# Ten of the twenty later modulation blocks summed on TensorE instead of VectorE, in a two-layer hybrid decoder on one Trainium2 core

## The chip, the cores and the metric

The kernel runs on one core of a Trainium2 chip. A core has five engines that run their own instruction streams: TensorE (PE in the profile, with PEld for the loading of its stationary operand), VectorE (DVE), ScalarE (ACT), GpSimd (POOL) and SyncE (SP), which here only issues DMA transfers. The metric is the device time of one execution in microseconds, as the median of several runs. The profile is of one execution, and its times are from the start of that execution's span.

## The reference, cut to what matters

The sequence has 256 tokens of 2048 channels. Each of two layers has a token-mixing part (one input projection, four groups of heads, one output projection) and a gated feed-forward part; both stand between normalisations that are modulated by vectors computed from one conditioning vector `c`:

```
cond = jax.nn.silu(c)
for l in range(DEPTH):
    mods = cond @ w_ada[l] + b_ada[l]
    sh1, sc1, g1, sh2, sc2, g2 = [m[:, None, :] for m in jnp.split(mods, 6, axis=-1)]
    h = rms_norm(x, norm_pre_mix[l]) * (1.0 + sc1) + sh1
    y = token_mixing(h, positions, w_in[l], w_out[l], ...)
    x = x + g1 * rms_norm(y, norm_post_mix[l])
    h = rms_norm(x, norm_pre_ffn[l]) * (1.0 + sc2) + sh2
    y = conv_ffn(h, ffn_w_in[l], ffn_conv_w[l], ffn_w_out[l])
    x = x + g2 * rms_norm(y, norm_post_ffn[l])
```

All is f32. `cond @ w_ada[l]` is a vector of 2048 times a matrix of 2048 x 12288, 100 MB a layer.

## The kernel before

**Weights and products.** A weight tile of 128 x 1024 f32 (512 KB) comes by DMA into the pool `raw` (4 buffers, line 406, on SP's queue). ScalarE rounds it into `wh` (line 423), VectorE takes the difference `wl` (line 424), and TensorE makes three products in its rounded f32 form for each one of the reference: activations high by weights high, high by low, low by high (`mm3`, line 228 is the matmul itself). Results gather in PSUM banks: four of the pool `mm`, and two each of two pools `mx`.

**The modulation blocks.** `mods` of a layer is cut into 12 blocks of 1024 columns, blocks 0 to 3 for the first normalisation, 4 and 5 for the first gate, 6 to 9 for shift and scale of the second normalisation, 10 and 11 for the second gate. Blocks 0 to 3 of layer 0 are computed at the start on TensorE, by `ada_quarter`. The other 20 blocks are background work, made by `ada`: 16 weight tiles of 128 x 1024, one after the other, come into the pool `rawa` (2 buffers, line 475), and VectorE multiplies each by its 128 values of `cond` and adds it to an accumulator (line 462; line 460 for the first). At the end a transpose (481), a reduction (483) and eight small matmuls sum over the 128 partitions.

**Order.** `wload` and `attn_probs` call `tick`, which at set rates starts the next background tile. With `paced` (in the feed-forward parts) the tile is held behind the last weight load; without it (mixers and output projection) the scheduler that orders each engine's stream at build time is free to place it. `drain` finishes what is left of a stage's blocks before the next stage. Ten blocks are unpaced: 4, 5, 8, 6, 9, 7 of layer 0 and 8, 6, 9, 7 of layer 1; ten are paced. In the output projection (`project_out`) all four `mm` banks are held by partial sums, twice, for one half of the columns each. After it `residual` (lines 683 to 701) computes the new x and its scale on VectorE, `pre_norm` brings h into `ht` by matmuls with `diag`, and the feed-forward matmuls begin; the second half of h needs blocks 7 and 9.

Each engine takes its instructions in the order in which they were placed.

Of the kernel before, what the change touches and what calls it, by code (L numbers as in the profile page):

```python
# [12 lines left out]
F32 = mybir.dt.float32  # L13
# [4 lines left out]
ALU = mybir.AluOpType  # L18
# [3 lines left out]
P = 128  # L22
D = 2048
S = 256
KT = D // P
# [167 lines left out]
class Ker:  # L193
# [273 lines left out]
    def ada(self, l, b):  # L467
# [19 lines left out]
                self.mm(cols[32 * q:32 * q + 32, :8], self.ident2[:, 32 * i:32 * i + 32], pv[:, :, q], i == 0, i == 1)  # L487
        self.ada_out(l, b, cols[:, :8])

    def ada_quarter(self, q):  # L490

        nc = self.nc
        bank = self.mx()
        pools = ((self.rawa, "rawa"), (self.rawm, "rawm"), (self.accp, "acc"))
        free = [A_OT + 1024] + (AT[7:9] if q else []) + (AT[:4] if q < 3 else [])
        for kc in range(KT):
            n = kc % (len(free) + 6)
            if n < len(free):  # L500
                w = self.reg(free[n], 1024)(1024)
            else:
                pool, nm = pools[(n - len(free)) % 3]
                w = pool.tile([P, 1024], F32, name=nm, tag=nm)
            nc.sync.dma_start(w, self.blk("w_ada", 0, kc, 1, (q * 512, 512), (D + q * 512, 512)))
            for i in range(2):
                o = 64 * (kc % 2) + 32 * i
                self.mm(bank[o:o + 32], self.condz[:, kc], w[:, i * 512:(i + 1) * 512], kc < 2, kc >= KT - 2)
            if kc % 2 and kc < KT - 1:
                yield  # L510
        with self.first():
            r = self.small.tile([P, 512], F32, name="hf", tag="hf")
            nc.scalar.copy(r, bank)
            cols = self.mx(8)
            for c in range(4):
                self.mm(cols[:, 2 * c:2 * c + 2], r[:, c * P:(c + 1) * P], self.ident2[:, 0:64:32], True, True)
            cols = cols.rearrange("p (c i) -> p i c", i=2)
            for i in range(2):
                self.ada_out(0, 2 * i + q // 2, cols[:, i], 4 * (q % 2))

    def ada_out(self, l, b, cols, j=0):

        nc = self.nc
        n = cols.shape[-1]
        out = self.mod[:, l, b, j:j + n]
        nc.vector.tensor_tensor(out, cols, self.vs(l, "b_ada")[:, b * 8 + j:b * 8 + j + n], op=ALU.add)
        which, part, half = b // 6, b % 6 // 2, b % 2
        g = 16 * which + 8 * half + j
        if part == 1:
            nc.vector.scalar_tensor_tensor(out, out, 1.0, self.vs(l, "pre")[:, g:g + n], op0=ALU.add, op1=ALU.mult)  # L530
        elif part == 2:
            nc.vector.tensor_tensor(out, out, self.vs(l, "post")[:, g:g + n], op=ALU.mult)

    def ada_blocks(self, l, blocks):
        for b in blocks:
            yield from self.ada(l, b)
            if b % 6 == 5:
                self.gate_out(l, b // 6)
            yield
# [1247 lines left out]
```

## Time and profile before

| | |
|---|---|
| median of 3 runs (lowest, highest) | 2699.17 us (2696.71, 2700.51) |
| the profiled execution | 2692.16 us, of it span 2690.0 us |
| mean granted TensorE clock | 0.978 |
| TensorE, VectorE, ScalarE busy | 96%, 71%, 47% of the span |
| mixers and output projection, layer 0 | about 150 to 630 us |
| feed-forward, layer 0 | about 630 to 1405 us |
| mixers and output projection, layer 1 | about 1405 to 1905 us |
| feed-forward, layer 1 | about 1905 to 2690 us |

The span is from the first to the last instruction. Times inside the program are read from a profile's own clock; a matmul's end is modelled, so that the start of one matmul to the start of the next says more of the pace than its length. An f32 matmul (not rounded) stands in the trace as two records. The granted clock is a share of TensorE's full speed: 1.00 is 2.4 GHz, 0.50 is 1.2 GHz, and values between are means over a stretch with both.

### The profile page before, as it was taken

The page shows a single profiled execution, that of the slowest core. Times are in us where ns is not written, and L with a number is a line of the kernel's source. Part 1 is how long each engine was busy: PE and PEld are TensorE (multiplying, and loading weights), DVE is VectorE, ACT ScalarE, POOL GpSimd, SP SyncE. Part 2 cuts the span into 40 slices and gives each one's busy share as a digit, 9 for nine tenths or more (in the row PEclk, how much of TensorE's full clock was granted, in tenths as well). Part 3 has the DMA queues.
Part 4 walks back from the last instruction along what each step waited for, and adds up shares of the span by engine and source line. Part 5 has one row for each costly group of instructions (what it writes and reads, how often), then busy time and mean ns, then how long its engine had stood idle before and what let it go on. Part 6 is the DMA issues. An engine that isn't in the chain of part 4 may idle for free. (4 is left out here: it accounts for less than half of the span.)

```text
span 2690.0 us, 44478 instructions
## 1 busy us (share of the span) xinstructions
PE 2571.7 (96%) x17604; PEld 2285.0 (85%) x17604; DVE 1910.7 (71%) x3014; ACT 1259.9 (47%) x2002; POOL 10.1 (0%) x22
## 2 busy tenths in 40 slices
PE   7979998888999999999998999999899999999998
PEld 4568786767999999988887879888899999998886
DVE  5568867878787778776877888865776655555555
ACT  3344454555445444454545445465544444444443
POOL 0000000000000000000000000000000000000000
PEclk9989998889999999999998999999999999999999
DMA  8765756676888888876676567735587655555554
GB/s 343 313 212 198 256 197 210 220 266 216 291 297 277 289 289 298 291 242 234 229 269 216 176 218 248 254 114 180 186 283 270 209 185 183 182 184 186 185 189 147
DMA packets 171264, 620.89 MB, mean 231 GB/s; under 512 B 19440, under 2 KB 20272, under 8 KB 169520
## 3 DMA queue, kind: packets, MB, share of 16 engines
q1 hardware_dynamic: 170048, 617.00, 67.1%
q8 instruction: 138, 2.26, 0.3%
q10 hardware_dynamic: 1008, 1.06, 0.1%
q14 instruction: 70, 0.57, 0.1%
HBM read 613.75 MB, written 4.23 MB: 230 GB/s over the span
## 5 line engine op out<-in xcount | busy, mean ns | idle before, releaser
L228 PE MATMUL mm<-ht,wh 128*128 128x256 f32 x7168 | 1314.9, 284 | 6.7 <-ACT ht L423 5.8
L423 ACT CAST wh<-raw 128x1024 fp32r<-128x1024 f32 (+1 forms) x740 | 771.5, 1043 | 960.9 <-PE mm L228 785.0
L424 DVE TENSOR_TENSOR wl<-raw,wh 128x1024 fp32r<-128x1024 f32 (+1 forms) x740 | 896.6, 1214 | 404.5 <-ACT wh L423 401.0
L228 PEld LDWEIGHTS mm<-ht,wh 128*128 128x128 f32 x7168 | 1112.3, 189 | 22.8 <-issue 7.6
L228 PE MATMUL mm<-ht,wl 128*128 128x256 f32 x3584 | 1018.1, 284 | 2.4 <-DVE wl L424 2.4
L228 PEld LDWEIGHTS mm<-ht,wl 128*128 128x128 f32 x3584 | 675.3, 188 | 10.5 <-DVE wl L424 6.2
L228 PE MATMUL mm<-wh,ht 128*128 128x512 f32 (+1 forms) x1600 | 508.0, 396 | 8.0 <-ACT ht L423 4.2
L462 DVE SCALAR_TENSOR_TENSOR acc<-rawa,condc,acc 128x1024 f32<-128x1024 f32 x300 | 384.6, 1282 | 138.2 <-DMA rawa<-in_w_ada_dram 136.8
L228 PEld LDWEIGHTS mm<-wh,ht 128*128 128x128 f32 x1600 | 303.1, 191 | 72.3 <-ACT ht L423 4.5
L228 PE MATMUL mm<-wl,ht 128*128 128x512 f32 (+1 forms) x800 | 316.2, 395 | 0.0
L228 PE MATMUL mx<-arena 128*128 128x128 f32 (+9 forms) x1576 | 235.1, 320 | 18.9 <-DVE arena L373 10.0
L228 PEld LDWEIGHTS mx<-arena 128*128 128x128 f32 (+5 forms) x1576 | 164.8, 169 | 72.5 <-issue 20.4
L228 PE MATMUL mx<-wh,ht 128*128 128x512 f32 x704 | 222.3, 396 | 0.0
L228 PEld LDWEIGHTS mm<-wl,ht 128*128 128x128 f32 x800 | 152.6, 191 | 31.5 <-issue 0.2
L228 PEld LDWEIGHTS mx<-wh,ht 128*128 128x128 f32 x704 | 132.6, 188 | 32.3
L228 PE MATMUL mx<-wl,ht 128*128 128x512 f32 x352 | 139.5, 396 | 0.0
L424 DVE TENSOR_TENSOR ht<-arena,ht 128x1024 fp32r<-128x1024 f32 x52 | 63.6, 1223 | 40.4 <-ACT ht L423 40.1
L1615 DVE SCALAR_TENSOR_TENSOR arena<-mm,vec,arena 128x255 f32<-128x255 f32 (+1 forms) x176 | 78.5, 478 | 6.2 <-ACT arena L1613 5.3
L423 ACT CAST ht<-arena 128x1024 fp32r<-128x1024 f32 x52 | 54.2, 1049 | 56.1 <-PE mm L228 30.5
L228 PEld LDWEIGHTS mx<-wl,ht 128*128 128x128 f32 x352 | 66.3, 188 | 16.2
L232 PE MATMUL mx<-ident,arena 128*128 128x128 f32 (+1 forms) x328 | 59.4, 287 | 13.4 <-ACT arena L815 5.5
L232 PEld LDWEIGHTS mx<-ident,arena 128*128 128x128 f32 (+1 forms) x328 | 38.4, 144 | 29.9 <-ACT arena L815 9.8
(314 smaller groups left out, 1516.4 us busy)
## 6 DMA issues: line engine op xcount, KB each, us to landing
raw<-in_ffn_w_in_dram SPq DMA_DIRECT2D x352, 512.0 KB, 4.2
rawa<-in_w_ada_dram SPq DMA_DIRECT2D x330, 512.0 KB, 5.0
raw<-in_ffn_w_out_dram SPq DMA_DIRECT2D x176, 512.0 KB, 4.3
raw<-in_w_in_dram SPq DMA_DIRECT2D x116, 512.0 KB, 4.3
raw<-in_w_out_dram SPq DMA_DIRECT2D x64, 512.0 KB, 4.1
arena<-in_w_ada_dram SPq DMA_DIRECT2D x36, 512.0 KB, 7.8
raw<-in_w_in_dram SPq DMA_DIRECT2D x32, 426.0 KB, 3.9
rawm<-in_w_ada_dram SPq DMA_DIRECT2D x9, 512.0 KB, 9.3
```

Source lines behind the costliest of these rows:

```text
L228: self.nc.tensor.matmul(out, lhsT=lhsT, rhs=rhs, start=start, stop=stop)
L232: self.nc.tensor.transpose(out, in_, self.ident[:k, :k])
L423: self.nc.scalar.copy(hi.bitcast(F32R), src)
L424: self.last_lo = self.nc.vector.tensor_sub(lo.bitcast(F32R), src, hi)
L462: self.nc.vector.scalar_tensor_tensor(acc, w, self.condc[:, kc:kc + 1], acc, op0=ALU.mult, op1=ALU.add)
L1615: nc.vector.scalar_tensor_tensor(c[:, s:], ps[m][:, :256 - s], self.fconv(l, 2 - s, f), c[:, s:], op0=ALU.mult, op1=ALU.add)
```

## The change

Unpaced blocks are computed by a new function, `ada_te`, the paced ones as before. A tile is now the moving operand of two f32 matmuls of 128 rows by 512 columns, whose stationary operand is one column of `cond` repeated 32 times: each writes 32 equal rows of a PSUM bank. Two tiles make a pair, whose four matmuls write the four groups of 32 partitions of one `mm` bank. ScalarE copies the first pair's bank into an accumulator of 128 x 512, VectorE adds the other seven. At the end of a block four matmuls with two columns of `ident2` add the two tiles' rows and turn them into columns. Tiles rotate over three buffers, two of `rawa` and one of `acc`.

```diff
+    def ada_te(self, l, b):
+        nc = self.nc
+        acc = self.acct()[:, 0:512]
+        tiles = []
+        for kc in range(KT + 1):
+            if kc and kc % 2 == 0:
+                bank = self.mmt()
+                for n, w in enumerate(tiles):
+                    for i in range(2):
+                        o = 64 * n + 32 * i
+                        k = kc - 2 + n
+                        self.mm(bank[o:o + 32], self.condc[:, k:k + 1].to_broadcast([P, 32]), w[:, i * 512:(i + 1) * 512],
+                                True, True)
+                if kc == 2:
+                    nc.scalar.copy(acc, bank)
+                else:
+                    nc.vector.tensor_tensor(acc, acc, bank, op=ALU.add)
+                tiles = []
+            if kc < KT:
+                pool, nm = ((self.rawa, "rawa"), (self.rawa, "rawa"), (self.accp, "acc"))[kc % 3]
+                tiles.append(pool.tile([P, 1024], F32, name=nm, tag=nm))
+                nc.sync.dma_start(tiles[-1], self.blk("w_ada", l, kc, 1, (b * 1024, 1024)))
+                yield
+        cols = self.mx(8)
+        for c in range(4):
+            self.mm(cols[:, 2 * c:2 * c + 2], acc[:, c * P:(c + 1) * P], self.ident2[:, 0:64:32], True, True)
+        self.ada_out(l, b, cols, order="c i")
...
     def ada_blocks(self, l, blocks):
         for b in blocks:
-            yield from self.ada(l, b)
+            yield from (self.ada if self.paced else self.ada_te)(l, b)
```

`ada_out` takes the other order of columns by a rearranged view. Lines behind the new function stand 30 to 33 lower: `residual` is at 716 to 734, the add of a pair at 508, a tile's load at 513.

**Where it moves instructions.** TensorE, layer 0, from the last product of the output projection (`mm<-wh,ht`) to the first of the feed-forward part (`mm<-ht,wh`); rows with `diag` are `pre_norm`'s. Before:

```order
L228 MATMUL mm<-wh,ht 128x512
L228 MATMUL mx_5511<-acc,ident_126 32x8 x8
L228 MATMUL mx_5524<-diag,arena 128x128
L228 MATMUL mx_5540<-diag,arena 128x128
L228 MATMUL mx_5524<-diag,arena 128x128 x3
L228 MATMUL mx_5540<-diag,arena 128x128 x3
L228 MATMUL mx_5550<-diag,arena 128x128 x4
L228 MATMUL mx_5560<-diag,arena 128x128 x4
L228 MATMUL mm<-ht,wh 128x256 x2
L228 MATMUL mm<-ht,wl 128x256
```

In the change, the end of the same stretch; `condc` marks the matmuls of pairs, whose tiles are in `rawa` or `acc`:

```order
L228 MATMUL mm<-acc,condc 32x512 x2
L228 MATMUL mm<-rawa,condc 32x512 x4
L228 MATMUL mm<-acc,condc 32x512 x2
L228 MATMUL mm<-rawa,condc 32x512 x4
L228 MATMUL mm<-acc,condc 32x512 x2
L228 MATMUL mm<-rawa,condc 32x512 x4
L228 MATMUL mm<-acc,condc 32x512 x2
L228 MATMUL mm<-rawa,condc 32x512 x4
L228 MATMUL mm<-acc,condc 32x512 x2
L228 MATMUL mm<-ht,wh 128x256 x2
L228 MATMUL mm<-ht,wl 128x256
L228 MATMUL mm<-ht,wh 128x256 x2
```

Thirty-eight matmuls of pairs (nine pairs and half of a tenth) now stand between the output projection's last product and the feed-forward part's first, the last 26 of them (rows 1 to 9) with nothing else between.

VectorE at the same place, where `residual` computes the scale that `diag` needs. Before:

```order
L272 SCALAR_TENSOR_TENSOR cy<-ca,cy 128x1 x2
L270 SCALAR_TENSOR_TENSOR ca<-cy,cv 128x1 x2
L272 SCALAR_TENSOR_TENSOR cy<-ca,cy 128x1 x2
L270 SCALAR_TENSOR_TENSOR ca<-cy,cv 128x1 x2
L272 SCALAR_TENSOR_TENSOR cy<-ca,cy 128x1 x2
L573 TENSOR_SCALAR diag<-ident,cy 128x128 x2
L701 SCALAR_TENSOR_TENSOR arena<-arena,cy 128x512 x4
```

In the change (508 is the add of a pair, 559 the end of block 9):

```order
L272 SCALAR_TENSOR_TENSOR cy<-ca,cy 128x1 x2
L270 SCALAR_TENSOR_TENSOR ca<-cy,cv 128x1 x2
L272 SCALAR_TENSOR_TENSOR cy<-ca,cy 128x1
L508 TENSOR_TENSOR acc<-acc,mm 128x512
L272 SCALAR_TENSOR_TENSOR cy<-ca,cy 128x1
L270 SCALAR_TENSOR_TENSOR ca<-cy,cv 128x1 x2
L272 SCALAR_TENSOR_TENSOR cy<-ca,cy 128x1
L559 TENSOR_TENSOR mod<-mx_5431,vec 128x8
L272 SCALAR_TENSOR_TENSOR cy<-ca,cy 128x1
L606 TENSOR_SCALAR diag<-ident,cy 128x128 x2
L734 SCALAR_TENSOR_TENSOR arena<-arena,cy 128x512 x4
```

An add that needs a pair's matmuls now stands in the middle of the scale's chain; there is another one earlier in it.

TensorE inside the mixers of layer 1, where a projection of 426 columns runs. Before:

```order
L228 MATMUL mm<-wl,ht 128x426
L228 MATMUL mm<-wh,ht 128x426 x2
L228 MATMUL mm<-wl,ht 128x426
L228 MATMUL mm<-wh,ht 128x426 x2
L228 MATMUL mm<-wl,ht 128x426
L228 MATMUL mm<-wh,ht 128x426 x2
L228 MATMUL mx_14208<-arena 64x128
```

In the change:

```order
L228 MATMUL mm<-wl,ht 128x426
L228 MATMUL mx_14382<-arena 128x128 x4
L228 MATMUL mm<-wh,ht 128x426 x2
L228 MATMUL mm<-wl,ht 128x426
L228 MATMUL mm<-wh,ht 128x426
L228 MATMUL mm<-rawa,condc 32x512 x2
L228 MATMUL mm<-acc,condc 32x512 x2
L228 MATMUL mm<-wh,ht 128x426
L228 MATMUL mm<-wl,ht 128x426
```

A pair stands between two matmuls of the projection, and the projection's matmuls behind it follow in the old order.

## Rows read from the trace of the kernel before

**Rows 1.** The page, busy time of each engine: us, share of the span, instructions

```profile
PE 2571.7 (96%) x17604; PEld 2285.0 (85%) x17604; DVE 1910.7 (71%) x3014; ACT 1259.9 (47%) x2002; POOL 10.1 (0%) x22
```

**Rows 2.** Busy time of each engine in six stretches, instructions, granted clock, DMA share

```profile
200.00:420.00 220.00, 217.75 (x1513) 185.90 (x1512) 178.15 (x340) 108.20 (x207) 0.52 (x1) 1.00 0.67 222
420.00:600.00 180.00, 151.38 (x894) 123.59 (x893) 139.75 (x322) 89.70 (x208) 3.23 (x3) 0.89 0.67 227
600.00:630.00 30.00, 30.00 (x144) 23.89 (x142) 23.03 (x24) 12.11 (x18) 0.00 (x0) 1.00 0.83 283
630.00:672.00 42.00, 32.81 (x273) 32.74 (x262) 35.56 (x78) 29.40 (x58) 0.00 (x0) 0.88 0.51 174
1500.00:1905.00 405.00, 401.91 (x2676) 340.25 (x2674) 297.88 (x611) 208.45 (x424) 0.53 (x1) 1.00 0.60 201
1905.00:1950.00 45.00, 36.31 (x292) 36.20 (x293) 37.32 (x81) 28.23 (x47) 0.00 (x0) 0.92 0.47 161
```

**Rows 3.** Who waited for whom, 1500 to 1905 us: us in total, times, longest

```profile
ACT wh L423 <- PE mm L228: 102.2, 59, 6.6
```

**Rows 4.** Waits of TensorE alone, 420 to 650 us

```profile
PE mx L228 <- DVE ry L256: 11.2, 2, 6.0
PE mx L228 <- issue: 9.2, 1, 9.2
```

**Rows 5.** Tile rawa: who waited for it; its loads, issue to landing

```profile
  PE mx L228: 7.0, 2
...
DMA to landing us min/median/max: 3.0/5.0/10.5
```

**Rows 6.** Groups by line and shape: count, then busy us and mean ns

```profile
L462 DVE SCALAR_TENSOR_TENSOR acc<-rawa,condc,acc 128x1024 f32<-128x1024 f32 x300 | 384.6, 1282 | 138.2 <-DMA rawa<-in_w_ada_dram 136.8
...
L481 DVE STREAM_TRANSPOSE acc<-acc 128x1024 f32<-128x1024 f32 x20 | 24.8, 1242 | 0.3
...
L483 DVE TENSOR_REDUCE acc<-acc 128x32 f32<-128x1024 f32 x20 | 24.2, 1212 | 0.0
...
L1395 DVE TENSOR_TENSOR arena<-mx,arena 128x512 f32<-128x512 f32 x32 | 21.5, 687 | 7.4 <-PE mx L228 7.2
```

**Rows 7.** TensorE in order of time near 92 us: start, us, what

```profile
92.09 0.28 PE L228 MATMUL mm<-ht,wl 128*128 128x256 f32 x1
92.30 0.62 PE L228 MATMUL mx<-arena 128*32 128x512 f32 x2
92.31 0.62 PE L228 MATMUL mx<-rawa,arena 128*32 128x512 f32 x2
...
93.30 0.50 PE L228 MATMUL mm<-ht,wh 128*128 128x256 f32 x2
93.73 1.04 PE L228 MATMUL mx<-rawm,arena 128*32 128x512 f32 x2
94.70 0.39 PE L228 MATMUL mm<-ht,wl 128*128 128x256 f32 x1
```

**Rows 8.** The chain that ended last, 1661 to 1668 us: start, us, what

```profile
1660.67 1.30 DVE acc L462
1661.99 4.08 DMA rawa<-in_w_ada_dram
```

**Rows 9.** TensorE in order of time, 628 to 646 us

```profile
628.75 0.63 PE L228 MATMUL mm<-wh,ht 128*128 128x512 f32 x2
629.22 0.40 PE L228 MATMUL mm<-wl,ht 128*128 128x512 f32 x1
...
639.30 5.96 PE L228 MATMUL mx<-diag,arena 128*128 128x128 f32 x32 [9.19 <-issue]
645.02 0.48 PE L228 MATMUL mm<-ht,wh 128*128 128x256 f32 x2
645.34 0.28 PE L228 MATMUL mm<-ht,wl 128*128 128x256 f32 x1
645.45 0.40 PE L228 MATMUL mm<-ht,wh 128*128 128x256 f32 x2
```

More of the change, by code (lines that the diff above doesn't have):

```diff
@@ L519, in ada_quarter, with ada_out @@
                 self.ada_out(0, 2 * i + q // 2, cols[:, i], 4 * (q % 2))
-    def ada_out(self, l, b, cols, j=0):
+    def ada_out(self, l, b, cols, j=0, order=None):
         nc = self.nc
@@ L525, in ada_out @@
         out = self.mod[:, l, b, j:j + n]
-        nc.vector.tensor_tensor(out, cols, self.vs(l, "b_ada")[:, b * 8 + j:b * 8 + j + n], op=ALU.add)
+        v = (lambda ap: ap) if order is None else (lambda ap: ap.rearrange("p (i c) -> p i c", i=2))
+        if order is not None:
+            cols = cols.rearrange("p (c i) -> p i c", i=2)
+        nc.vector.tensor_tensor(v(out), cols, v(self.vs(l, "b_ada")[:, b * 8 + j:b * 8 + j + n]), op=ALU.add)
         which, part, half = b // 6, b % 6 // 2, b % 2
```

## The prediction

> **What bounds the kernel now.** I read the busy times by stretch first, because the change touches only the mixers and output projections, and a mean over 2690 us mixes them with the feed-forward parts. From 200 to 420 us TensorE is busy 217.75 of 220 us, from 1500 to 1905 us 401.91 of 405, both at granted clock 1.00, that is 2.4 GHz; VectorE is busy 178.15 and 297.88, 81% and 74% [rows 2]. The table of waits says the same from the other side: in the second stretch the longest entry is ScalarE waiting for TensorE to free a weight buffer, 102.2 us in 59 waits [rows 3]. So there TensorE sets the pace, and what VectorE does for a modulation block lies beside it.
>
> One stretch is different. From 420 to 600 us TensorE is busy 151.38 of 180 us, 28.6 idle, at a mean clock of 0.89 [rows 2]. With levels 1.00 and 0.50, 0.89 means 22% of 180 us, about 40, at half clock, which loses about 20 us of full-speed work. Between 420 and 650 TensorE waits 11.2 us for VectorE (line 256) in two waits, and once 9.2 us before `pre_norm`'s matmuls, with nothing that the profile shows as releaser [rows 4]; that one stands just ahead of 639.30, between output projection and feed-forward [rows 9]. Over the whole span TensorE is at 96%, VectorE at 71% [rows 1].
>
> **The change part by part.**
>
> *Removed from VectorE.* A block costs it 15 multiply-adds of 1.28 us, one first tile at about the same, a transpose of 1.24 and a reduction of 1.21: 22.9 us; ten blocks 229. Added are seven adds of 128 x 512 out of PSUM; the nearest row, 0.69 us [rows 6], makes 4.8 a block, 48 in ten. Net VectorE loses about 180 us of work. It lies beside a TensorE that is 99% busy in two of the three stretches and pays only where TensorE waits for VectorE (d). ScalarE gains one copy a block, at 47% busy [rows 1]: nothing. The same 160 tiles of 512 KB are loaded.
>
> *(a) TensorE's added passes.* One pass is up to four 512-wide f32 matmuls in the four column blocks. Where the kernel already does this, the four start within 10 ns (the rows at 92.30 and 92.31, two records each) and the next matmul starts at 93.30: 1.00 us, and 1.21 from the matmul ahead, 1.09 when its usual 0.12 is taken off. One column block alone takes 93.73 to 94.70, 0.97 [rows 7]. So four cost what one costs, and a pair that the order breaks in two pays twice. Ten blocks make 80 pairs, 48 in layer 0 and 32 in layer 1; in the new order they stand in 114 passes, as some pairs have another matmul inside. At 1.03 that is 117 us, and about 4 more for the four small matmuls that end a block (they replace eight smaller ones): **+121**. Bounds: all pairs whole and 0.4 lost per block end, 80 x 1.09 + 4 = 91; 114 x 1.09 + 4 = 128. TensorE has no room for this in the full stretches, so it goes into the time.
>
> *(b) Waits for tiles.* TensorE takes its instructions in order, so a pair whose tile has not landed holds every matmul behind it; VectorE, which has room, could wait for a tile at no cost, and did: 136.8 us for `rawa` in line 462 [rows 6]. With three buffers for pairs of two, a pair's second tile can be loaded only when the first tile of the pair before has been used. The period of a pair is then one pass, 1.0, and one landing. A landing is 3.0 us at least and 5.0 at the median [rows 5]; the one in the chain that ended last took 4.08 after the accumulation that freed its buffer [rows 8]. I take 5.0 as the period, with 4.0 and 6.0 as bounds. Where TensorE has 5 us of other work between one pair's start and the next's, the wait is nothing; where it has less, the rest is lost. I went through the new order and priced the work between pairs at 0.11 us for a 256-wide matmul, 0.235 for a 512-wide one, 0.18 for a `diag` one [rows 9] and 1.0 for a pass: 34 of the 80 pairs have less than 5 us. The missing work sums to **96** (67 at a period of 4, 132 at 6): mixers of layer 0 22 (9 pairs), the boundary between the halves of its output projection 9.5 (3), the stretch behind it 34.5 (10); in layer 1 18.5 (7), 8 (4) and 3.5 (1). The clumps are there because a pair needs an `mm` bank and the output projection holds all four: pairs that came due meanwhile stand together at its half and its end.
>
> The Trainium skill, "TensorE: Matmul & The Clock Gate", Part 3, "What overlaps and what doesn't", speaks against the change here: matmuls start and end strictly in program order. If matmuls could pass one another, the sum would lose this term, and by the rule it keeps it; TensorE's 7.0 us in two waits for `rawa` tiles [rows 5] agree.
>
> Behind a held pair in layer 0 stand `residual`'s scale (VectorE's add of a pair is in the middle of that chain, so it waits for the pair too) and then the whole feed-forward. On SP's queue a tile's load now waits for TensorE where it waited for VectorE; weight loads stand behind it. Four `raw` buffers hold some 11 us of products (24 matmuls of 0.12 a tile), more than a period, so I cost this at nothing; with that cover gone it is a period, 5 us, each time.
>
> *(c) Cover.* Part of (b) falls into idle time that was there already: the 9.2 us before `diag`, 3.5 of the 8.7 us that TensorE is idle from 1905 to 1950, and in 420 to 600 the 28.6 idle less the 11.2 that (d) takes, 17 [rows 2, 4]: **-30**.
>
> *(d) What VectorE's relief gives.* The 11.2 us of waits for VectorE could go, and with less waiting some of the half clock. Before, the clock fell where TensorE had been waiting; the new pairs make waits of their own there, so I take half of the 20 us: **-21** (bounds -11 and -31; nothing at all if the add in the chain is as late as what left it).
>
> Sum: 121 + 96 - 30 - 21 = +166. The profiled execution was 2692.16, 7.0 under the median 2699.17; that makes 2858 on its scale and 2865 on the median's. I forecast **2860**.
>
> **The rivals.**
>
> 1. As above, 2860; with the bounds of (a) and of the period (91 and 67, 128 and 132) 2806 to 2908, and 2800 to 2915 as its own range. Chance 0.62.
>
> 2. The tile waits are hidden: loads are early enough, or fall into idle time. Then passes alone count: 121 - 21 - 10 for passes that fall into idle time = +90, or 91 - 21 - 10 = +60 with cheap passes: 2759 to 2789, about 2770. For it: landings of 3.0 exist, and tiles may come while TensorE does long work. Against: the buffer, not the queue, holds the load back. 0.17.
>
> 3. The other side, faster: TensorE is not full, its busy time hides short waits for VectorE's rounding. Weight loads were busy 185.90 of 220 us and 340.25 of 405, 99 us less than the stretches [rows 2]. If all of that were such waits and left with VectorE's work, then with passes in the middle of their bounds 106 - 99 - 21 = -14, 2685. It decides only if the tile waits net of cover stay under 9 us, which wants a period of about 3 us, no more than the shortest landing alone. Against it: from 600 to 630 us TensorE is busy 30.00 of 30 and the loads 23.89, 80% as well [rows 2], with nothing waited for, so the share belongs to the shape of the matmuls; and ScalarE's 102.2 us of waiting for TensorE [rows 3] says that the rounded weights are early. 0.07.
>
> The Trainium skill, "Perfetto Trace Analysis", "Identifying the Most-Contended Engine", calls TensorE's matmul share a poor measure of its room and the share of the weight loads a good one. By that rule the mixers have 15 to 16% of room and the time is this rival's 2685.
>
> 4. Clumps are worse: a period of 6, and half clock after each wait, so that the passes of those 34 pairs cost twice and the clock part of (d) is gone: 121 + 132 + 35 - 30 - 11 = +247, 2946. For it: the clock was 0.88 and 0.92 in the two transitions of before, where TensorE waits [rows 2]. 0.12.
>
> 5. All cancels, 2699: 0.02. That the blocks stay on VectorE is excluded by the order, which shows the pairs.
>
> **How the numbers follow.** 0.2%, 5.4 us, is about what a measurement of this kernel can tell from no change. Faster by more is rival 3, 0.07; within it rival 5, 0.02; slower the other three, 0.91. For the range I leave out below 2755 rivals 3 and 5 and a little of 2, above 2930 most of rival 4: about 0.2 in all.
>
> **What the profile after would show.** For (a): 160 tiles as 32 x 512 matmuls, a whole pair's four starts within tens of ns and 1.0 us to the next matmul; about 1.0 apart each time where a pair is broken. For (b): TensorE's table of waits led by loads of `rawa` and `acc`, some 34 waits, under 100 us together; the longest gap between output projection and feed-forward in layer 0, 15.8 us before (629.22 to 645.02 [rows 9]), about 50 after. Layer 0's mixers take about 90 us more, layer 1's about 75, the feed-forward parts the same within a few us. For (d): line 256's 11.2 us gone from TensorE's waits. VectorE's busy time falls by about 180.
>
> It would be wrong if tiles land well before their pair in the clumps (TensorE's waits for loads under 30 us: rival 2), if the old matmuls of the mixers come closer together than before at full clock (rival 3), or if the clock stays at 0.5 through the clumps (rival 4).

## The result, and the profile after

The changed kernel took 2954.07 us (median of 4 runs, 2948.94 to 2962.74) against 2698.02 before, a ratio of 1.0952 (95% interval 1.0931 to 1.0972): 256 us slower, where 162 were forecast, 24 us above the range. Its profiled execution has a span of 2950.8 us.

The page of the profile after, busy time of each engine, beside [rows 1]:

```profile
PE 2769.2 (94%) x18164; PEld 2340.1 (79%) x18164; DVE 1773.4 (60%) x2904; ACT 1269.3 (43%) x2014; POOL 10.2 (0%) x22
```

VectorE is busy 137 us less and TensorE 198 us more. The stages tell where the time went. I take layer 0's mixers from 150 us to the first feed-forward matmul (row 645.02 in [rows 9], 802.50 below), layer 1's from the last matmul of layer 0's feed-forward to the first of layer 1's:

| stage, us in the profiled execution | before | after | more |
|---|---|---|---|
| layer 0, mixers to feed-forward | 495.0 | 652.5 | 157.5 |
| feed-forward, layer 0 | 770.5 | 773.8 | 3.3 |
| layer 1, mixers to feed-forward | 503.3 | 603.3 | 100.0 |
| feed-forward, layer 1 | 758.9 | 758.9 | 0 |

So nearly all of it lies where the change is, as said; but layer 0 should have lost about 90 and layer 1 about 75. The same two stages whole, layer 0 and layer 1 before, then layer 0 and layer 1 after, in the columns of [rows 2]:

```profile
150.00:645.02 495.02, 447.44 (x2816) 375.97 (x2814) 389.70 (x814) 239.98 (x492) 3.93 (x5) 0.94 0.66 221
1415.52:1918.83 503.31, 478.23 (x3204) 411.76 (x3202) 378.56 (x800) 261.28 (x528) 1.05 (x2) 0.98 0.59 197
150.00:802.50 652.50, 564.19 (x3131) 406.50 (x3125) 308.46 (x750) 243.47 (x495) 3.93 (x5) 0.88 0.50 167
1576.27:2179.53 603.26, 555.75 (x3428) 436.29 (x3426) 324.02 (x755) 266.27 (x532) 1.05 (x2) 0.93 0.50 164
```

TensorE's idle time grows by 63 us (length less busy time). Of its busy time, half clock costs 63 us more than before, worked out from the granted clock in each busy piece. The remaining 131 us are more work, counted at full clock; the matmuls of pairs are 121 of them. The forecast had the 121, and 45 for all the rest.

Stretches of layer 0 after, in the columns of [rows 2] (us; busy PE, PEld, DVE, ACT, POOL; granted clock; DMA share; GB/s):

```profile
200.00:420.00 220.00, 179.45 (x1049) 125.48 (x1048) 108.46 (x264) 77.36 (x159) 0.53 (x1) 0.88 0.40 134
420.00:600.00 180.00, 160.26 (x929) 122.15 (x928) 61.97 (x186) 58.45 (x127) 0.96 (x1) 0.84 0.41 137
...
757.20:802.50 45.30, 27.89 (x110) 8.92 (x108) 21.07 (x66) 4.96 (x10) 0.00 (x0) 0.81 0.69 243
```

From 200 to 420 us TensorE was busy 217.75 of 220 us with 1513 instructions at full clock; it is now busy 179.45 with 1049, at 0.88, and the DMA engines move 134 GB/s for 222. TensorE is not overfull there: it has too little to do. TensorE in order of time at the end of the emptiest piece (start, us, what, in brackets the idle time ahead and its releaser):

```profile
343.64 0.66 PE L232 MATMUL mx<-ident,arena 128*128 128x128 f32 x4 [0.73 <-ACT arena L1210]
345.03 1.16 PE L228 MATMUL mx<-arena 128*128 128x128 f32 x8 [0.73 <-ACT arena L1161]
346.97 1.16 PE L228 MATMUL mx<-arena 128*128 128x128 f32 x8 [0.78 <-DVE arena L1130]
...
349.35 0.95 PE L228 MATMUL mx<-ident,acc 128*128 128x2 f32 x8
350.65 0.56 PE L228 MATMUL mx<-arena 32*32 32x32 f32 x16 [0.35 <-DVE mod L559]
...
358.73 1.92 PE L228 MATMUL mm<-acc,condc 128*32 128x512 f32 x2
360.58 1.22 PE L228 MATMUL mx<-arena 128*128 128x128 f32 x4
361.73 0.62 PE L228 MATMUL mm<-acc,condc 128*32 128x512 f32 x1
361.74 0.62 PE L228 MATMUL mm<-rawa,condc 128*32 128x512 f32 x2
...
362.72 0.50 PE L228 MATMUL mm<-ht,wh 128*128 128x256 f32 x2
```

These are links of a group of heads' recurrence: each small matmul waits 0.7 us for ScalarE or VectorE, which waited for the matmul ahead. Before, projections (`mm<-ht,wh`) filled such waits; from 233 to 362.72 us there is now none, and again none from 405 to 475. (Before, the longest piece without one in these mixers is 427.9 to 479.9.) The row at 349.35 is the end of an old modulation block (its accumulator turned into columns). The rows at 358.73 and 361.73 are a pair of the next block: one of its four matmuls stands alone at 358.73, with a link of the recurrence behind it, and the other three start at 361.73. Right behind that pair the projections resume. SyncE's waits (150 to 760 us: who waited for whom, us in total, times, longest) and its transfers in order of time:

```profile
SPq L513 <- PE mm L228: 108.6, 44, 9.3
SPq L513 <- PE mx L228: 90.3, 6, 48.0
```

```profile
297.89 4.34 SPq L454 DMA_DIRECT2D rawm<-in_mla_w_uq_dram  x2
350.33 12.80 SPq L513 DMA_DIRECT2D acc<-in_w_ada_dram  x2
363.23 0.39 SPq L513 DMA_DIRECT2D rawa<-in_w_ada_dram  x1
371.42 0.33 SPq L406 DMA_DIRECT2D raw<-in_w_in_dram  x1
```

Nothing is issued for 48.0 us until 350.33: the next tile goes into the pool of the accumulators, whose two buffers are then the new block's accumulator and the old block's, and the load starts when the matmuls at 349.35 have freed the latter. The next longest of the six waits is 36.6 us, until 461.91. That is a loss the prediction doesn't have. Two of its own rows, TensorE's waits after (whole span), and the run up to the feed-forward of layer 0:

```profile
PE mm L228 <- DMA acc<-in_w_ada_dram: 23.3, 10, 5.7
PE mm L228 <- DMA rawa<-in_w_ada_dram: 22.2, 13, 3.8
```

```profile
777.13 0.62 PE L228 MATMUL mm<-acc,condc 128*32 128x512 f32 x2 [1.67 <-DMA acc<-in_w_ada_dram]
...
784.72 1.92 PE L228 MATMUL mm<-acc,condc 128*32 128x512 f32 x4 [5.68 <-DMA acc<-in_w_ada_dram]
...
789.94 1.05 PE L228 MATMUL mm<-acc,condc 128*32 128x512 f32 x4 [1.11 <-DMA acc<-in_w_ada_dram]
...
802.50 0.50 PE L228 MATMUL mm<-ht,wh 128*128 128x256 f32 x2
```

Pairs wait for tiles in the clump as expected, but they wait 45.5 us in 23 waits over the whole kernel, half of what I took before cover.

### The profile page after: what moved, and what is told of

Same layout as the page of the kernel before. It is cut to its first block, busy times and chain, and to the rows that moved or that the text cites. A ratio compares the mean times of both kernels' runs of the same rounds, so it can differ in the third digit from the quotient of the medians.

```text
span 2950.8 us, 45519 instructions
## 1 busy us (share of the span) xinstructions
PE 2769.2 (94%) x18164; PEld 2340.1 (79%) x18164; DVE 1773.4 (60%) x2904; ACT 1269.3 (43%) x2014; POOL 10.2 (0%) x22
## 4 chain that ended last, share of the span: by engine, by line
PE 88%; DVE 5%; DMA 3%; ACT 3%; issue 1%; SPq 0%; ACTq 0%; DVEq 0%
PE mm L228 65%; PE mx L228 21%; PE mx L232 2%; DMA acc<-in_w_ada_dram 1%; DMA rawa<-in_w_ada_dram 1%; DVE wl L424 1%; DVE arena L1130 1%; ACT wh L423 1%; ACT junk L693 0%; DVE arena L1428 0%; DMA arena<-in_w_ada_dram 0%; DMA vec<-in_vec_dram 0%; ACT arena L1161 0%; DVE ca L270 0%; ACT arena L1210 0%
## 5 line engine op out<-in xcount | busy, mean ns | idle before, releaser
L228 PE MATMUL mx<-arena 128*128 128x128 f32 (+8 forms) x1576 | 251.3, 333 | 38.6 <-DVE gea L1101 9.5
L228 PEld LDWEIGHTS mx<-arena 128*128 128x128 f32 (+5 forms) x1576 | 177.1, 181 | 97.7 <-issue 28.1
L462 DVE SCALAR_TENSOR_TENSOR acc<-rawa,condc,acc 128x1024 f32<-128x1024 f32 x150 | 192.2, 1281 | 54.5 <-DMA rawa<-in_w_ada_dram 53.5
L228 PE MATMUL mm<-rawa,condc 128*32 128x512 f32 x440 | 113.6, 674 | 24.6 <-DMA rawa<-in_w_ada_dram 22.2
L508 DVE TENSOR_TENSOR acc<-acc,mm 128x512 f32<-128x512 f32 x70 | 47.9, 685 | 117.7 <-PE mm L228 117.1
L228 PE MATMUL mm<-acc,condc 128*32 128x512 f32 x200 | 73.7, 693 | 24.6 <-DMA acc<-in_w_ada_dram 23.3
L232 PE MATMUL mx<-ident,arena 128*128 128x128 f32 (+1 forms) x328 | 66.5, 316 | 29.6 <-DVE arena L1130 11.1
```

The costliest lines, as they stand in the source:

```text
L228: self.nc.tensor.matmul(out, lhsT=lhsT, rhs=rhs, start=start, stop=stop)
L232: self.nc.tensor.transpose(out, in_, self.ident[:k, :k])
L462: self.nc.vector.scalar_tensor_tensor(acc, w, self.condc[:, kc:kc + 1], acc, op0=ALU.mult, op1=ALU.add)
L508: nc.vector.tensor_tensor(acc, acc, bank, op=ALU.add)
```

## Experiments

The runs compare with before on the same chip (its median there was 2700 to 2704 us). The change itself was not run again there: differences from it take its 2954, measured where before took 2698, so in ratios they come out 5 to 9 us larger. Stage times are from each run's own profiled execution; that of before took 2692, some 10 us less than its medians here, so stage differences from before add up to other sums than the medians'. The streams are put in order at build for each kernel anew, so that a stage can differ for that alone; by how much was not measured.

**Theories.** A, the queue: tile loads on SyncE's queue hold weight loads behind them. B, the shared buffer: the tile that waits for the old block's end keeps its pair from running; the pair holds one of the four `mm` banks, which are given out in turn, and so the projections behind it. C, the prediction's: passes and tile waits alone.

**Own queue.**

```diff
-                nc.sync.dma_start(tiles[-1], self.blk("w_ada", l, kc, 1, (b * 1024, 1024)))
+                nc.gpsimd.dma_start(tiles[-1], self.blk("w_ada", l, kc, 1, (b * 1024, 1024)))
```

> The tile loads of the ten changed blocks are issued by GpSimd's queue in place of SyncE's; all else as in the change (2954). Theory A, the queue: on SyncE's queue a tile load that waits for TensorE (199 us in 50 waits in layer 0) holds the weight loads behind it, so that projections are late; freed of it the time falls by half of what the change cost or more, to 2800 to 2860. Theory B, the shared buffer: the tile that comes into the accumulators' pool waits for the end of the block before, its pair holds a PSUM bank in its turn, and the projections behind need that bank; the queue does not matter: 2935 to 2970. Theory C, the prediction's: passes and tile waits spread over the clumps: 2940 to 2965.

2961.98 us, ratio to before 1.096 (1.0919 to 1.100). TensorE's order is nearly that of the change, the tile loads now wait on a queue that carries no other transfer, and the time is no shorter. A falls.

**Own buffer.**

```diff
-        acc = self.acct()[:, 0:512]
+        acc = self.small.tile([P, 512], F32, name="hf", tag="hf")
```

> The accumulator of a block gets a 128 x 512 buffer of its own (of the pool of small tiles), so that both buffers of the accumulators' pool are there for tiles: four tile buffers where there were three. Theory B: the waits of 48.0, 36.7 and 22.2 us on SyncE's queue for the accumulators' pool go, and with them the stretches of layer 0 in which the chain of small matmuls stands without a projection beside it (233 to 363 and 405 to 475 us): 2820 to 2870. Theory A gives the same here, by another way. Theory C: the fourth buffer shortens some tile waits, 45 us in all, by half: 2930 or a little less.

2835.15 us, 1.0489 (1.0464 to 1.0513): 119 us of the 256 are back. It also leaves four buffers for tiles where there were three, so that it doesn't test the sharing alone. Layer 0 takes 556.4 us, layer 1 574.7. TensorE's first wait is for tiles, and no longer for the old block:

```profile
PE mm L228 <- DMA rawa<-in_w_ada_dram: 24.6, 14, 3.9
```

**Few loads.** The difference to the change:

```diff
-                pool, nm = ((self.rawa, "rawa"), (self.rawa, "rawa"), (self.accp, "acc"))[kc % 3]
-                tiles.append(pool.tile([P, 1024], F32, name=nm, tag=nm))
-                nc.sync.dma_start(tiles[-1], self.blk("w_ada", l, kc, 1, (b * 1024, 1024)))
+                if kc < 2:
+                    keep.append(self.rawa.tile([P, 1024], F32, name="rawa", tag="rawa"))
+                    nc.sync.dma_start(keep[-1], self.blk("w_ada", l, kc, 1, (b * 1024, 1024)))
+                tiles.append(keep[kc % 2])
```

> Each changed block loads two tiles and uses them for all eight pairs (so its modulation values are not the reference's): all passes, copies and adds, no waiting for tiles and no load from the third on. What is left over the time before is the passes' own price less VectorE's relief. The prediction's terms (a) and (d) give 2699 + 121 - 21 = 2799, with 10 of it hidden 2789. Theory C: the rest of the change, 155 us, was tile waits. If passes cost more than about 1 us each, or break the old order by themselves, it stays over 2850.

2760.15 us, 1.0206 (1.0186 to 1.0226): better than 2789, and far from 2850. With the waiting for tiles and most loads left out, 194 of the 256 us are gone.

**No blocks.** `ada_te` yields sixteen times and ends with

```diff
+        self.mm(cols, self.ident, self.ident2[:, 0:8], True, True)
+        self.ada_out(l, b, cols, order="c i")
```

> The ten blocks are left out on every engine: no loads, no sums, only the last addition with a small matmul in place of the sum (so the modulation values are not the reference's). It shows what the mixers take without this work. The prediction's (d), 21 us for VectorE's relief, gives 2678 against 2699, and with 80 MB fewer to load perhaps 2665. If TensorE's busy time in the mixers hides waits for VectorE (the prediction's rival 3, 99 us), it is 2600 or less.

2639.2 us, 0.976 (0.9738 to 0.9781): 64 us, three times the 21 of the prediction. Layer 0 goes from 495.0 to 443.3 us, layer 1 only from 503.3 to 497.3. The stretch from 420 to 600 us, to be read against [rows 2] (151.38 busy, clock 0.89):

```profile
420.00:600.00 180.00, 171.46 (x1043) 148.78 (x1043) 111.39 (x289) 109.54 (x228) 2.27 (x2) 0.97 0.45 143
```

Both the idle time of TensorE and the half clock are nearly gone, though with layer 0 shorter the stretch holds somewhat later work. Few loads less no blocks is 2760.15 - 2639.2 = 121 us: the price of the passes with the block ends, copies and adds, and of two loads a block.

**Other bank.**

```diff
-                bank = self.mmt()
+                bank = self.mx()
```

> A pair's matmuls write a bank of the mx pools in place of one of the four mm banks; the tile buffer shared with the accumulator stays as in the change. Theory B as it stands after the first four runs: a pair that waits for its tile (itself waiting for the old block's end) holds an mm bank in turn, and the projections that need the banks after it stand behind. Then without the mm bank the naked chains of layer 0 go although the buffer is still shared: 2840 to 2880. If the shared buffer alone does it, through the tile and the matmuls in order, the time stays at 2930 or more.

2819.71 us, 1.0438 (1.0422 to 1.0454), 134 us less than the change although the buffer is still shared. TensorE's waits in layer 0's mixers are led by the tiles, and the waits for ScalarE and VectorE of the recurrence no longer stand at the top:

```profile
PE mx L228 <- DMA rawa<-in_w_ada_dram: 14.4, 4, 7.1
PE mx L228 <- DMA acc<-in_w_ada_dram: 10.8, 8, 2.5
PE mx L232 <- ACT arena L848: 4.5, 1, 4.5
```

The projections get on again: from 200 to 480 us ScalarE rounds 50 weight tiles (line 423) in the kernel before, 22 in the change, 36 with the own buffer and 48 here. Undoing either half of the knot frees the projections. Here the pairs have three buffers as in the change, so a fourth one is not what helps. B stands, and it takes the buffer and the bank together.

**Loads unread.** As few loads, with

```diff
+                else:
+                    nc.sync.dma_start(self.accp.tile([P, 1024], F32, name="acc", tag="acc"), self.blk("w_ada", l, kc, 1, (b * 1024, 1024)))
```

> As with two loaded tiles a block (2760), and the other 14 tiles are loaded too, into the accumulators' pool, but nothing reads them (modulation values not the reference's). It tells whether the 75 us between 2760 and the change with its own buffer (2835) are the transfers (memory traffic and places on SyncE's queue) or the pairs' waiting for them. Transfers: 2810 to 2840. Waits of pairs: 2755 to 2780.

2805.03 us, 1.0386 (1.0368 to 1.0404), just under the range for transfers and well over the one for waits: 45 us over few loads. In layer 1 it costs nothing (545.9 against 545.5), in layer 0 27 us and in its feed-forward part 16. These loads take turns with the accumulators, so the run has part of the knot in it, and the two layers differ: it doesn't settle what transfers cost.

**Buffer and queue.** Own buffer and own queue together.

> The accumulator with a buffer of its own, and the tile loads on GpSimd's queue. If, with the shared buffer gone, weight loads stand behind tile loads that wait for TensorE on SyncE's queue, the time falls from 2835 to 2780 to 2805; if the rest is pairs that wait for tiles, it stays at 2825 to 2845.

2844.62 us, 1.0534 (1.0507 to 1.056): no gain over the buffer alone. A is out here too.

**One block.** With the own buffer,

```diff
-            yield from (self.ada if self.paced else self.ada_te)(l, b)
+            yield from (self.ada_te if (l, b) == (0, 9) and not self.paced else self.ada)(l, b)
```

> Only block 9 of layer 0 on TensorE, with the accumulator's own buffer; the other nine on VectorE as before. From the runs: a block costs TensorE 12.5 us and 6.5 of waiting; leaving out all six blocks of layer 0 gave 52 us, 8.7 each if even: then 10 slower than before, 2713. If the relief lies mostly in the stretch from 420 to 600 us, where this block runs, it is 15 to 25 and the time 2688 to 2700.

2749.47 us, 1.0182 (1.0164 to 1.02): a miss by 36 us or more. The reason is in TensorE's waits from 150 to 720 us:

```profile
PE mx L228 <- DVE acc L483: 34.7, 1, 34.7
```

Block 7, on VectorE, comes after block 9, which stood in the clump at the end of the output projection; it began too late, and the feed-forward waited 34.7 us for its reduction.

**VectorE with few loads, and loads alone.** In the kernel before, `ada` loads two tiles a block and uses them again; in the kernel without blocks, all 160 tiles are loaded:

```diff
-            w = self.rawa.tile([P, 1024], F32, name="rawa", tag="rawa")
-            self.nc.sync.dma_start(w, self.blk("w_ada", l, kc, 1, (b * 1024, 1024)))
+            if self.paced or kc < 2:
+                w = self.rawa.tile([P, 1024], F32, name="rawa", tag="rawa")
+                self.nc.sync.dma_start(w, self.blk("w_ada", l, kc, 1, (b * 1024, 1024)))
+                keep.append(w)
+            else:
+                w = keep[kc % 2]
```

```diff
         for kc in range(KT):
+            self.nc.sync.dma_start(self.rawa.tile([P, 1024], F32, name="rawa", tag="rawa"), self.blk("w_ada", l, kc, 1, (b * 1024, 1024)))
             yield
```

> The kernel before with all of VectorE's work, but each of the ten blocks loads two tiles and uses them eight times (modulation values not the reference's). Leaving the blocks out gave 63 us, 52 of it in layer 0. If that was VectorE's work: 2690 to 2705, no gain. If it was the transfers (memory traffic, places on SyncE's queue, waits for tiles): 2640 to 2660.

> No block is summed on any engine, but all 160 tiles are loaded into their two buffers, unread (modulation values not the reference's). The other half of the same question: VectorE's work as the cause: 2640 to 2655, as without blocks; transfers as the cause: 2685 to 2705.

2704.84 us, 1.0005 (0.9994 to 1.0016), and 2645.96 us, 0.9786 (0.9763 to 0.981). The stretch from 420 to 600 us, VectorE with few loads first, then loads alone:

```profile
420.00:600.00 180.00, 138.80 (x852) 114.31 (x853) 131.81 (x326) 88.25 (x212) 3.23 (x3) 0.86 0.26 83
```

```profile
420.00:600.00 180.00, 171.37 (x1055) 148.41 (x1053) 109.71 (x287) 109.90 (x230) 2.27 (x2) 0.97 0.58 191
```

At 83 GB/s TensorE still is busy only 138.80 us; at 191 GB/s, without VectorE's sums, 171.37. So the 64 us are VectorE's work (59 between these two runs) and the loads are worth some 7. By layers, the mixers of layer 0 take 509.7 us with VectorE's sums and 444.9 with the loads alone, those of layer 1 495.2 and 504.6: in layer 1 VectorE's sums cost nothing.

**Buffer and bank.** Both mends.

> Both mends together: the accumulator's own buffer, and the pairs' bank from the mx pools. Alone they gave 2835 (layer 0 556 us, layer 1 575) and 2820 (572 and 552). If the two losses are different ones, about 2790 to 2805, with the 2760 of the two-tile kernel as the floor; if both break the same knot, 2815 to 2835. In either case slower than before.

2803.17 us, 1.0359 (1.0331 to 1.0387). With both, 43 us are left over few loads, and 151 us less than the change. The two mends gave 119 and 134 singly, so it is mostly one knot, with a smaller part of its own in each. The 43 us are for the most part not waits for tiles. TensorE's idle time ahead of pairs' matmuls is 10.5 us here and 7.1 in few loads, while the pairs take 121 us of TensorE at full clock here and 97 there, because more tiles run by themselves (counted from each start of a pair's matmul to TensorE's next start, idle time taken off).

**Before, with its own queue.** `ada`'s unpaced loads on GpSimd's queue.

> The kernel before, with the tile loads of the ten unpaced blocks on GpSimd's queue: can the 52 us of layer 0 be had without moving the sums? If tile loads that wait for VectorE (62.5 us in 47 waits in layer 0's mixers) hold weight loads back on SyncE's queue: 2680 to 2693. If not, within 8 us of before, as the own queue did nothing for the changed kernel.

2756.27 us, 1.0188 (1.0159 to 1.0217): 52 us slower, in both layers (522.9 and 528.9). I had expected a gain or nothing. Whether the queue itself or the other order at build (some 5% of TensorE's rows stand elsewhere) does it was not tried.

**First two blocks, first block.** Both mends, with only blocks 4 and 5 of layer 0, or 4, on TensorE.

> Blocks 4 and 5 of layer 0 alone on TensorE, with the accumulator's own buffer and the pairs' bank from the mx pools; the other eight on VectorE. Theory even: passes cost 12 a block, waits about 4, VectorE's relief in layer 0 is 8.7 a block whichever blocks leave: 2 x 7 slower, 2710 to 2725. Theory first blocks: VectorE is in the way only when it is nearly full, so the first blocks that leave it give most of the 52 us: 2680 to 2695, faster than before.

> Block 4 of layer 0 alone, as above. Theory even: 2703 + 7 = 2710. Theory first blocks: a relief of 20 to 26 for one block against 16: 2692 to 2700.

2720.74 us, 1.0061 (1.0039 to 1.0084), and 2712.99 us, 1.0036 (1.0019 to 1.0052): 20 and 13 us slower by the medians, as the even theory had it. But with one block the last product of the output projection starts at 629.65 us, before at 629.46: up to there the block costs nothing. The loss lies behind it:

```profile
647.13 3.97 PE L228 MATMUL mx<-diag,arena 128*128 128x128 f32 x16 [17.08 <-issue]
...
661.28 0.28 PE L228 MATMUL mx<-acc,ident 128*32 128x8 f32 x2 [6.21 <-DVE acc L483]
```

The wait ahead of `diag` is 17.08 us where it was 9.2 [rows 4], and there is a new one of 6.21 for the reduction of a block on VectorE, as in one block. With two blocks the last product starts at 640.86 and these waits are 17.2 and 6.8. So these runs don't show how the relief is spread over the blocks; no run took the late VectorE block out of that place. No version here that computes all the blocks beats the kernel before.

## Why the prediction was wrong, step by step

The sum from the runs: 2703 before, -64 without the blocks, +121 for the passes, +43 for what both mends leave, +151 for the knot, makes 2954. Each term is the difference of two runs, so the sum must come out; what each is made of has to be read from the traces. The prediction's was +121 for passes, +96 - 30 for tile waits, -21 for relief.

- **(a) Passes: right in size.** In the changed kernel the pairs take 144 us of TensorE with idle time taken off, 121 counted at full clock; 117 was forecast, and 4 for block ends. That few loads less no blocks is 121 as well is partly luck: its pairs take 97, and the rest is what hangs on them. A whole pair takes 1.00 us:

```profile
190.91 0.62 PE L228 MATMUL mm<-acc,condc 128*32 128x512 f32 x2
190.92 0.62 PE L228 MATMUL mm<-rawa,condc 128*32 128x512 f32 x2
191.36 0.60 PE L228 MATMUL mm<-acc,condc 128*32 128x512 f32 x2
191.38 0.60 PE L228 MATMUL mm<-rawa,condc 128*32 128x512 f32 x2
191.91 0.46 PE L228 MATMUL mm<-wh,ht 128*128 128x426 f32 x1
```

- **(b) and (c) Tile waits: the mechanism right, the size too large.** 96 was taken before cover; TensorE's waits for pairs' tiles come to 45.5 us in the changed kernel, and its idle time ahead of pairs with both mends (four buffers instead of three) to 10.5. The period was the lower bound, 4, and not 5: between 777.13 and 802.50 run the last 26 matmuls of pairs, six and a half pairs in 25.4 us, 3.9 us a pair. The gap ahead of layer 0's feed-forward is 45.3 us (757.2 to 802.5), about 50 was said.
- **The step that failed** is in (b): "Where TensorE has 5 us of other work between one pair's start and the next's, the wait is nothing". It looked at each pair and the work ahead of it, and took the work for the same as before. It saw that "a pair needs an `mm` bank" only where the output projection holds all four, and not the reverse, that a pair which waits holds a bank against the projections. Nor did it see that the third tile buffer is a block's accumulator, so that a new block's first tile there waits for the old block's end. The order after shows it without any time: in layer 0's mixers 494 records of TensorE in a row belong to no projection (233.5 to 362.2 us) and another 239 (405.4 to 474.5); the longest such run before has 337, with the own buffer 162 and with the other bank 266. A recurrence without projections runs at the pace of its waits and, as the clock of 0.88 and 0.84 shows, partly at half clock. That is the 151 us: with both mends, idle time in the two stages of mixers falls by 87 us, and what half clock costs in busy time by 69 (counted as in the result), while pairs and the rest take 10 more (146 in sum between the two profiled executions). Rival 4 had a number near the result (2946) for another reason in the main, a longer period and half clock in the clumps; the half clock was there, but most of it in the mixers.
- **SyncE's queue at nothing: right**, though the profile shows 199 us of its waits for TensorE. On its own queue they cost the same.
- **(d) Relief: the mechanism right, mis-sized.** 21 taken, bounds 11 and 31; 64 measured, 59 of it VectorE's work. The two waits named VectorE for 11.2 us only, but nearly all of the stretch's 28.6 idle us and 20 us of half clock hung on it: without the blocks the stretch is busy 171.46 at 0.97. Its place was right, 52 of it lie in layer 0. VectorE's groups of instructions lost about what was worked out: 192.4 for the multiply-adds against +47.9 for the adds, 176 in all. A block's first tile took 0.75 us, not 1.28. The busy time on the page, in which instructions that overlap count once, fell by 137 and not by 180.
- **Rival 3 (faster): its condition was not met, its reason half.** In layer 1 leaving out the blocks gave 6 us, and the share of the weight loads stayed where it was, 297.06 of 350:

```profile
1500.00:1850.00 350.00, 348.95 (x2292) 297.06 (x2291) 193.00 (x460) 181.63 (x381) 0.53 (x1) 1.00 0.42 136
```

  The Trainium skill, "Perfetto Trace Analysis", "Identifying the Most-Contended Engine", by which the weight loads' 84% there would be room, is not borne out in that stretch: the 65 us that they were short of it [rows 2] were no waits for VectorE's blocks. (The rival's 106 is not the middle of 91 and 128, which is 109.5; its number would be 2689.)

Without the knot the forecast would have been high by some 57 us (2860 against 2803): the relief was taken 43 too small and the other terms together 23 too large (187 against 121 + 43), 66 in all, less 9 from my rounding and the lower median of before.

## What to carry to other kernels

When background work moves to another engine, list every buffer and bank that it takes a turn in, and who takes the next turn: a wait in a side job that holds one of four PSUM banks stops the main work behind it, and neither the table of that engine's waits nor the load queue shows it as such. Compare the orders not only for where the new instructions stand, but for what has left the places where chains of small matmuls wait. To size what an engine's relief is worth, leave its work out in a run; the waits that name it gave a sixth of the answer.

## What was not expected of the hardware

- GpSimd's queue is no free way out: the own queue changed nothing for the changed kernel (2962 against 2954) and made the kernel before 52 us slower; the cause is open.
- A pass takes 1.00 us at full clock with all four matmuls of a pair (190.91 to 191.91), and 1.85 at half clock with a single one (358.73 to 360.58, granted clock 0.50). In the clump ahead of layer 0's feed-forward, after waits for tiles, TensorE in order of time:

```profile
767.16 1.92 PE L228 MATMUL mm<-rawa,condc 128*32 128x512 f32 x4
769.01 2.29 PE L228 MATMUL mx<-diag,arena 128*128 128x128 f32 x9
```

That pass, of one tile, has 1.85 us too (767.16 to 769.01, clock 0.50). So a pass there can cost nearly double, as rival 4 had it, but in this stretch the mean clock was 0.81. Over the whole kernel half clock made the pairs 24 us longer (144.3 against 120.6); rival 4 had 35.
